# A DiT block with SSD and RG-LRU branches on one core: modulation one tile ahead, scans and Silus at other places

## The chip, the cores and the metric

One core of a Trainium2 chip. The metric is the device time of one execution in microseconds. TensorE (PE) multiplies matrices, VectorE (DVE) and ScalarE (ACT) work element by element, SyncE (SP) issues the loads, and 16 DMA engines carry them. Each engine executes its own instructions in the order in which they stand.

## The reference

One layer over 256 latent tokens with 256 context tokens, width 2048, fp32. Cut to what the change touches:

```python
mod = jax.nn.silu(c) @ w_ada + b_ada              # shift, scale and gate vectors
h = modulate(rmsnorm(x, norm_mix), sh_m, sc_m)    # h * (1 + scale) + shift
z, xs, bs, cs, dt_raw, xr, yr = split(h @ w_in)   # one input projection
# RG-LRU branch: r, i = sigmoid(gates(conv(xr))); a = exp(-8 * r * softplus(-lam))
#   u = sqrt(1 - a**2) * i * xr; bidirectional linear scan of (a, u)
# SSD branch: xs, bs, cs = silu(conv(...)); dt = softplus(dt_raw + bias)
#   y = chunked scan with exp(cumsum(dt * A)), 32 heads, 4 groups
out = (g_s * (ssd @ w_out_ssd) + g_r * (lru @ w_out_lru)) @ w_o
x = x + g_m * out; then modulate, SwiGLU FFN, gated residual, final rmsnorm
```

The context tokens use the same weights, and of them only the final states of the two scans are needed.

## The kernel before

Channels lie on the 128 partitions, so the width is 16 tiles (KT = 16); latent and context tokens stand side by side in 512 columns. Weights arrive in fp32 and are split on the chip: ScalarE casts a high part `wh` from `raw`, VectorE subtracts to a low part `wl`. A product is three matmuls: high by high, high by low, low by high. The activations have the same two parts, `T1` and `T2`.

**First stage (L324 to L413).** X is loaded and squared, and the sums of squares give `r1`, the reciprocal root mean square. Then for each tile k: `ada_sums(k)` multiplies the conditioning vectors by the modulation weights of the tile (four loads `wa` of 512 KB, 32 small matmuls, L344), `ada_turn(k)` copies the sums (`ra`) and transposes them, `modulated(k)` works out scale and shift, then `tt` (VectorE, L371), `T1` (ScalarE, L372) and `T2` (VectorE, L373). `slice_prep(k)` loads a weight slice `raw0` of 448 KB (seven column blocks, L381) and splits it into `wh0` and `wl0`. `main(k)` multiplies seven column blocks, three matmuls each (L391 to L393): a group below is such a block's three matmuls. The first stage's TensorE and SyncE orders are those of the program text; the orders of ScalarE and VectorE are chosen by the scheduler. `wa` has six buffers.

**Later stages.** `run` works through jobs (a weight block of 128 columns each). Behind every job's evacuation it runs one list of `turns` (`in_turn(n, f)` puts f n jobs ahead) and one step of the background list `bg`. In the LRU stage two tiles make a batch (`lru_batch`): `operands`, `gates` (matmuls `lg`, Sigmoids), `decays` (Exp and Tanh) and `scans` (Sqrt of `E`, then the scans). In the SSD stage six jobs (xs x4, B, C) make a group; behind the last one come the Silus of B, C and XS, the transposes (`pB`, `px`), the product `pC`, and four units. A unit fetches the cumulated decays (`AC`), builds `E` and `G` (L804, L813), takes two exponentials, multiplies (`operands`), and feeds 24 small matmuls `py` (`products`, L833).

ScalarE holds one set of function tables at a time, and changing the set is an instruction of its own (ACT_TABLE_LOAD, recorded at L107). `fn` (L105) chains all activations that need tables in the order of the program text.

Of the kernel before, what the change touches and what calls it, by code (L numbers as in the profile page):

```python
# [8 lines left out]
F32 = mybir.dt.float32  # L9
# [46 lines left out]
def hybrid_block(  # L56
# [62 lines left out]
    def lru_ps(name):  # L119
        return ps_tile("lru", name, 2)  # L120
# [206 lines left out]
    ssq = lru_ps("ssq")  # L327
    for k in range(0, KT, 2):
        sq = sp.tile([P, 2, 2 * T], F32, tag="sq2", name="sq", bufs=2)
        act.activation(sq, X[:, k:k + 2, :], AF.Square)  # L330
        dve.tensor_tensor(sq[:, 0], sq[:, 0], sq[:, 1], ALU.add)
        pe.matmul(ssq, ones, sq[:, 0], start=k == 0, stop=k == KT - 2)
    r1 = rstd_of(ssq, 2 * T, "r1", sp)
# [3 lines left out]
    def ada_sums(j):  # L337

        pa = ras[j] = lru_ps("pa")
        for q in range(4):  # L340
            w = sp.tile([P, 4, 2 * P], F32, tag="wa", name="wa", bufs=6)
            nc.sync.dma_start(w, w_ada_m[j, :, 4 * q:4 * q + 4, :])
            for g in range(4):
                pe.matmul(pa[32 * g:32 * g + 32, :2 * P], C[:, 4 * q + g, :], w[:, g, :],  # L344
                          start=q == 0, stop=q == 3, tile_position=(0, 32 * g))
# [10 lines left out]
    def modulated(j):  # L356
# [11 lines left out]
        for s in range(2):  # L368
# [4 lines left out]
            dve.scalar_tensor_tensor(T2[:, j, sl], tt[:, sl], sh, T1[:, j, sl].bitcast(F32),  # L373
                                     ALU.add, ALU.subtract)
# [20 lines left out]
    with tc.manual_schedule(engines={mybir.EngineType.PE, mybir.EngineType.SP}):  # L395
        ada_sums(0)
        ada_turn(0)
        hl = {0: slice_prep(0)}
        modulated(0)
        ada_sums(1)  # L400
        ada_turn(1)
        for k in range(KT):
            if k + 1 < KT:
                hl[k + 1] = slice_prep(k + 1)
                modulated(k + 1)
            main(k, range(5))
            if k + 2 < KT:
                ada_sums(k + 2)
            main(k, range(5, N0))
            if k + 2 < KT:  # L410
                ada_turn(k + 2)
            del hl[k]
# [3 lines left out]
    dve.tensor_scalar(lt[3], col("lam", 0, 32), -1.0, None, ALU.mult)  # L416
# [92 lines left out]
    def lru_batch(tiles):  # L509
# [42 lines left out]
        def scans():  # L552
# [4 lines left out]
            for t in tiles:  # L557
# [15 lines left out]
        todo = [(False, [lambda: operands(t0)]), (False, before[:]), (False, [lambda: gates(t0), lambda: operands(t1)]),  # L573
                (False, []), (True, [lambda: gates(t1), decays])]
# [23 lines left out]
    def dt_evac(ps):  # L598
# [13 lines left out]
        def steps(part):  # L612
# [11 lines left out]
            if part == 0:  # L624
# [9 lines left out]
                fn(ex[:, :P], ex[:, :P], AF.Exp)  # L634
                dve.tensor_tensor(ex[f, :P], ex[f, :P], dt[f, 0:P], ALU.mult)
                dve.tensor_tensor(ex[b, :P], ex[b, :P], dt[b, P:2 * P], ALU.mult)
                cols = (dt[:, :P], dt[:, P:], ac[:, :P], ac[:, P:], ex[:, :P])
            else:
                scan(ex[f, :T - 1][:, ::-1], da[f, 1:][:, ::-1], T - 1, f)
                scan(ex[b, 1:], da[b, :T - 1], T - 1, b)  # L640
                fn(ex, ex, AF.Exp)
                dve.tensor_tensor(ex, ex, dt, ALU.mult)
                cols = (ex[:, :P], ex[:, P:])

# [14 lines left out]
            return turn  # L659

        def first():
            turn0()
            in_turn(4, steps(1))

        turn0 = steps(0)
        in_turn(4, first)

# [24 lines left out]
    LONG = ((1, 2, 3), (4, 5, 6, 7), (2, 3, 4, 5), (3, 4, 5, 6))  # L692
    SHORT = ((2, 3, 5), (7, 9, 11, 13), (4, 6, 7, 9), (5, 7, 9, 11))

    def xs_evac(g, t):
        def f(ps):
# [6 lines left out]
            if t == 3:  # L703
                silus, *rest = ssd_group(g)
                silus()
                for ns, fs in zip(LONG if g < NG - 1 else SHORT, rest):
                    for n, part in zip(ns, fs):
                        in_turn(n, part)
        return f

    def ssd_group(g):
# [133 lines left out]
        return (silus, [context_tokens, context_states, carried_states], *zip(*units))  # L845
# [277 lines left out]
```

## Time and profile before

| | |
|---|---|
| time, median of 3 runs | 2028.81 us (2024.41 to 2029.35) |
| profiled execution | 2027.59 us, span 2025.8 us |
| mean granted clock of TensorE | 0.986 |
| busy: TensorE, VectorE, ScalarE | 97%, 71%, 54% of the span |
| DMA | 440.32 MB, mean 217 GB/s |
| table loads | 48 at L107, 1283 ns each |

The first stage ends about 139 us into the span, the LRU stage at some 520, the SSD groups at some 850; behind them come the remaining projections and the FFN. The span is that of the profiled execution; it is 1.8 us shorter than the execution's own time.

### The profile page before, as it was taken

How to read it: one execution, taken by the hardware profiler on the slowest of the kernel's cores; microseconds unless marked ns; L12 is line 12 of the kernel's file. 1: busy time of each engine (PE TensorE's matmuls, PEld its weight loads, DVE VectorE, ACT ScalarE, POOL GpSimd, SP SyncE). 2: the span in 40 equal slices, each digit the busy share in tenths (PEclk: the TensorE clock that was granted, in tenths of full speed). 3: DMA queues.
4: the chain of work that ended last, by engine and by line, in shares of the span. 5: the costliest groups of instructions: out<-in, count | busy, mean ns of one | idle time of the engine just before them, and what ended most of it. 6: DMA issues, size and time to landing. Idle time of an engine off the chain costs nothing.

```text
span 2025.8 us, 30510 instructions
## 1 busy us (share of the span) xinstructions
PE 1963.7 (97%) x11633; PEld 1691.9 (84%) x11633; DVE 1430.7 (71%) x2153; ACT 1088.2 (54%) x1652; POOL 0.2 (0%) x4
## 2 busy tenths in 40 slices
PE   7999899999999879999999999899999999999997
PEld 3778898898878769888888888788888888888887
DVE  5578989886776666888777878776666665545544
ACT  4245878684564454766655544554444444444442
POOL 0000000000000000000000000000000000000000
PEclk9999999999999989999999999999999999999999
DMA  9974354556454457899888877577777776666663
GB/s 371 358 271 144 122 160 132 170 170 199 140 160 143 138 164 228 264 315 360 290 274 274 271 249 254 175 249 232 231 241 237 230 230 189 184 188 186 185 193 122
DMA packets 143842, 440.32 MB, mean 217 GB/s; under 512 B 17488, under 2 KB 36176, under 8 KB 143568
## 3 DMA queue, kind: packets, MB, share of 16 engines
q1 hardware_dynamic: 143328, 437.91, 66.4%
q8 instruction: 91, 1.49, 0.3%
q10 hardware_dynamic: 368, 0.47, 0.1%
q14 instruction: 55, 0.45, 0.1%
HBM read 427.77 MB, written 10.55 MB: 216 GB/s over the span
## 4 chain that ended last, share of the span: by engine, by line
PE 92%; DMA 2%; DVE 2%; ACT 2%; issue 1%; SPq 0%; DVEq 0%; ACTq 0%
PE ps L206 36%; PE ps L209 19%; PE ps L188 5%; PE ps L189 5%; PE ps L190 5%; PE ps L192 3%; PE ps L193 3%; PE ps L194 3%; DMA AC<-acD 1%; PE ps L391 1%; PE pa L344 1%; PE ps L392 1%; PE py L833 1%; PE ps L393 1%; PE ps L228 1%; PE lg L535 1%
## 5 line engine op out<-in xcount | busy, mean ns | idle before, releaser
L174 DVE TENSOR_TENSOR wl<-raw,wh 128x1024 fp32r<-128x1024 f32 (+1 forms) x566 | 677.8, 1200 | 386.9 <-ACT wh L173 382.3
L173 ACT CAST wh<-raw 128x1024 fp32r<-128x1024 f32 (+1 forms) x566 | 581.0, 1030 | 646.8 <-issue 221.4
L206 PE MATMUL ps<-T,wh 128*128 128x512 f32 x3236 | 814.7, 393 | 0.0
L206 PEld LDWEIGHTS ps<-T,wh 128*128 128x128 f32 x3236 | 581.6, 189 | 105.2 <-issue 0.7
L209 PEld LDWEIGHTS ps<-T,wl 128*128 128x128 f32 x3236 | 442.7, 190 | 33.3
L209 PE MATMUL ps<-T,wl 128*128 128x256 f32 x3236 | 452.9, 282 | 0.0
L188 PE MATMUL ps<-T,wh 128*128 128x512 f32 x464 | 184.2, 397 | 0.0
L189 PE MATMUL ps<-T,wh 128*128 128x512 f32 x464 | 180.9, 390 | 0.0
L190 PE MATMUL ps<-T,wl 128*128 128x512 f32 x464 | 180.6, 389 | 0.0
L473 DVE SCALAR_TENSOR_TENSOR rawa<-rawa,sc 128x1024 f32<-128x1024 f32 x128 | 153.1, 1222 | 28.4 <-DMA rawa<-in_dram 28.1
L192 PE MATMUL ps<-T,wh 128*128 128x256 f32 x576 | 165.4, 287 | 0.0
L193 PE MATMUL ps<-T,wh 128*128 128x256 f32 x576 | 163.7, 284 | 0.0
L194 PE MATMUL ps<-T,wl 128*128 128x256 f32 x576 | 163.6, 284 | 0.0
L192 PEld LDWEIGHTS ps<-T,wh 128*128 128x128 f32 x576 | 111.3, 193 | 1.9 <-issue 0.7
L193 PEld LDWEIGHTS ps<-T,wh 128*128 128x128 f32 x576 | 111.4, 193 | 1.2 <-issue 0.5
L194 PEld LDWEIGHTS ps<-T,wl 128*128 128x128 f32 x576 | 111.2, 193 | 0.0
L188 PEld LDWEIGHTS ps<-T,wh 128*128 128x128 f32 x464 | 87.1, 188 | 20.5 <-issue 2.3
L189 PEld LDWEIGHTS ps<-T,wh 128*128 128x128 f32 x464 | 87.2, 188 | 18.9 <-issue 1.4
L190 PEld LDWEIGHTS ps<-T,wl 128*128 128x128 f32 x464 | 87.1, 188 | 18.5
L107 ACT ACT_TABLE_LOAD x48 | 61.6, 1283 | 0.8
L804 ACT ACTIVATE E<-AC,wt 128x128 f32<-128x128 f32 x64 | 20.6, 391 | 61.8 <-DMA AC<-acD 61.8
L385 DVE TENSOR_TENSOR wl<-raw,wh 128x896 fp32r<-128x896 f32 x16 | 17.5, 1092 | 45.1 <-ACT wh L384 45.1
(236 smaller groups left out, 1881.8 us busy)
## 6 DMA issues: line engine op xcount, KB each, us to landing
raw<-in_dram SPq DMA_DIRECT2D x534, 512.0 KB, 4.5
rawa<-in_dram SPq DMA_DIRECT2D x128, 512.0 KB, 5.9
wa<-in_dram SPq DMA_DIRECT2D x64, 512.0 KB, 7.2
AC<-acD SPq DMA_DIRECT2D x16, 512.0 KB, 6.6
raw<-in_dram SPq DMA_DIRECT2D x16, 448.0 KB, 7.1
raw<-in_dram SPq DMA_DIRECT2D x16, 384.0 KB, 3.3
raw<-in_dram SPq DMA_DIRECT2D x18, 256.0 KB, 2.7
X<-in_dram SPq DMA_DIRECT2D x8, 512.0 KB, 7.2
```

Of the source, the lines that this page charges most:

```text
L107: i = act.activation(dst, src, func, **kw).ins
L173: act.copy(h[:, :n], raw[:, :n])
L174: held["low"] = dve.tensor_sub(l[:, :n], raw[:, :n], h[:, :n].bitcast(F32)).ins
L188: pe.matmul(ps, wh, T1[:, k, :], start=s, stop=False)
L189: pe.matmul(ps, wh, T2[:, k, :], start=False, stop=False)
L190: pe.matmul(ps, wl, T1[:, k, :], start=False, stop=e)
L192: pe.matmul(ps[:, :T], wh, T1[:, k, :T], start=s, stop=False)
L193: pe.matmul(ps[:, :T], wh, T2[:, k, :T], start=False, stop=False)
L194: pe.matmul(ps[:, :T], wl, T1[:, k, :T], start=False, stop=e)
L206: pe.matmul(ps, wh, job.act(k), start=s, stop=False, skip_group_check=True)
L209: pe.matmul(ps[:, T:], l[:, i % KP, :], job.act(i)[:, :T], start=False, stop=i == last, skip_group_check=True)
L473: i = dve.scalar_tensor_tensor(raw, raw, 1.0, sc[:, h * 1024:h * 1024 + 1024], ALU.mult, ALU.mult, accum_out=MP[:, n, h:h + 1]).ins
```

## The change

Five pieces. (1) The squares go through the four `raw` buffers instead of two of their own, and stand ahead in the hand-written order; the Sqrt table is loaded early; the reciprocal is taken in two halves. (2) `wa` gets a seventh buffer, and sums, turn and modulation of a tile are done one tile ahead of its `main` instead of two; the groups of `main(k)` are spread around them. The softplus of `lam` waits for the modulation of tile 8. (3) In the LRU stage the `scans` of the batch before move from ahead of `gates(t0)` to behind it. (4) The softplus and scans of dt are spread over more turns. (5) The Silus of an SSD group go into the turn list behind the job, where the exponentials of the last unit of the group before stand already, instead of straight into the evacuation; and of the group before the last the last unit's products come one turn later.

```diff
@@ -324,13 +324,20 @@
     dve.memset(C, 0.0)
     fn(C[:, :, 0], col("c", 0, KT), AF.Silu)
     fn(C[:, :, 1], col("cc", 0, KT), AF.Silu)
-    ssq = lru_ps("ssq")
-    for k in range(0, KT, 2):
-        sq = sp.tile([P, 2, 2 * T], F32, tag="sq2", name="sq", bufs=2)
-        act.activation(sq, X[:, k:k + 2, :], AF.Square)
-        dve.tensor_tensor(sq[:, 0], sq[:, 0], sq[:, 1], ALU.add)
-        pe.matmul(ssq, ones, sq[:, 0], start=k == 0, stop=k == KT - 2)
-    r1 = rstd_of(ssq, 2 * T, "r1", sp)
+    fn(junk, epsb[:, 0:1], AF.Sqrt)
+    r1 = sp.tile([P, 2 * T], F32, name="r1")
+
+    def square_sums():
+
+        ssq = lru_ps("ssq")
+        for k in range(0, KT, 2):
+            sq = wp.tile([P, 2, 2 * T], F32, tag="raw", name="sq", bufs=RING)
+            act.activation(sq, X[:, k:k + 2, :], AF.Square)
+            dve.tensor_tensor(sq[:, 0], sq[:, 0], sq[:, 1], ALU.add)
+            pe.matmul(ssq, ones, sq[:, 0], start=k == 0, stop=k == KT - 2)
+        fn(r1, ssq, AF.Sqrt, bias=epsb[:, 0:1], scale=1.0 / D)
+        for s in range(2):
+            dve.reciprocal(r1[:, s * T:s * T + T], r1[:, s * T:s * T + T])
 
     ras = {}
 
@@ -338,7 +345,7 @@
 
         pa = ras[j] = lru_ps("pa")
         for q in range(4):
-            w = sp.tile([P, 4, 2 * P], F32, tag="wa", name="wa", bufs=6)
+            w = sp.tile([P, 4, 2 * P], F32, tag="wa", name="wa", bufs=7)
             nc.sync.dma_start(w, w_ada_m[j, :, 4 * q:4 * q + 4, :])
             for g in range(4):
                 pe.matmul(pa[32 * g:32 * g + 32, :2 * P], C[:, 4 * q + g, :], w[:, g, :],
@@ -370,8 +377,9 @@
             sc, sh = MA[:, s, j:j + 1], MA[:, 2 + s, j:j + 1]
             dve.scalar_tensor_tensor(tt[:, sl], X[:, j, sl], sc, r1[:, sl], ALU.mult, ALU.mult)
             act.activation(T1[:, j, sl], tt[:, sl], AF.Identity, bias=sh)
-            dve.scalar_tensor_tensor(T2[:, j, sl], tt[:, sl], sh, T1[:, j, sl].bitcast(F32),
-                                     ALU.add, ALU.subtract)
+            i = dve.scalar_tensor_tensor(T2[:, j, sl], tt[:, sl], sh, T1[:, j, sl].bitcast(F32),
+                                         ALU.add, ALU.subtract)
+        held["mod", j] = i.ins
 
 
     ps0 = [mm_ps("ps0") for _ in range(3)] + [lru_ps("ps0")] + [ssd_ps("ps0") for _ in range(3)]
@@ -393,27 +401,29 @@
             pe.matmul(ps0[n], l[:, n, :], T1[:, k, :], start=False, stop=k == KT - 1)
 
     with tc.manual_schedule(engines={mybir.EngineType.PE, mybir.EngineType.SP}):
+        square_sums()
         ada_sums(0)
         ada_turn(0)
         hl = {0: slice_prep(0)}
         modulated(0)
-        ada_sums(1)
-        ada_turn(1)
         for k in range(KT):
+
+            n = (N0, 4, 2)[k] if k < 3 else 1
+            main(k, range(n))
             if k + 1 < KT:
+                ada_sums(k + 1)
                 hl[k + 1] = slice_prep(k + 1)
+                main(k, range(n, min(n + 1, N0)))
+                ada_turn(k + 1)
                 modulated(k + 1)
-            main(k, range(5))
-            if k + 2 < KT:
-                ada_sums(k + 2)
-            main(k, range(5, N0))
-            if k + 2 < KT:
-                ada_turn(k + 2)
+            main(k, range(n + 1 if k + 1 < KT else n, N0))
             del hl[k]
 
 
     lt = [sp.tile([P, 32], F32, name=f"lt{i}") for i in range(4)]
-    dve.tensor_scalar(lt[3], col("lam", 0, 32), -1.0, None, ALU.mult)
+    i = dve.tensor_scalar(lt[3], col("lam", 0, 32), -1.0, None, ALU.mult).ins
+    tc.add_manual_dep(i, held["mod", 8].name, mybir.DependencyInfo(
+        mybir.DependencyClass.NoSync, mybir.DependencyReason.DATA), reason="first tiles first")
     log1p_exp(lt[3], lt[3], lt[:3])
     for i, m in enumerate((-LRU_C, LRU_C)):
         dve.tensor_scalar(SL[:, i, :], lt[3], m, None, ALU.mult)
@@ -570,8 +580,8 @@
 
 
         t0, t1 = tiles
-        todo = [(False, [lambda: operands(t0)]), (False, before[:]), (False, [lambda: gates(t0), lambda: operands(t1)]),
-                (False, []), (True, [lambda: gates(t1), decays])]
+        todo = [(False, [lambda: operands(t0)]), (False, []),
+                (False, [lambda: gates(t0), lambda: operands(t1)] + before), (False, []), (True, [lambda: gates(t1), decays])]
         before[:] = [scans]
         if tiles[1] == KT - 1:
             todo.append((False, [scans]))
@@ -631,16 +641,20 @@
                 for c in range(2):
                     for d, pr in enumerate((f, b)):
                         side.dma_start(acD[c, d], ac[pr, c * P:c * P + P])
-                fn(ex[:, :P], ex[:, :P], AF.Exp)
-                dve.tensor_tensor(ex[f, :P], ex[f, :P], dt[f, 0:P], ALU.mult)
-                dve.tensor_tensor(ex[b, :P], ex[b, :P], dt[b, P:2 * P], ALU.mult)
                 cols = (dt[:, :P], dt[:, P:], ac[:, :P], ac[:, P:], ex[:, :P])
             else:
                 scan(ex[f, :T - 1][:, ::-1], da[f, 1:][:, ::-1], T - 1, f)
                 scan(ex[b, 1:], da[b, :T - 1], T - 1, b)
-                fn(ex, ex, AF.Exp)
-                dve.tensor_tensor(ex, ex, dt, ALU.mult)
                 cols = (ex[:, :P], ex[:, P:])
+
+            def weights():
+                if part == 0:
+                    fn(ex[:, :P], ex[:, :P], AF.Exp)
+                    dve.tensor_tensor(ex[f, :P], ex[f, :P], dt[f, 0:P], ALU.mult)
+                    dve.tensor_tensor(ex[b, :P], ex[b, :P], dt[b, P:2 * P], ALU.mult)
+                else:
+                    fn(ex, ex, AF.Exp)
+                    dve.tensor_tensor(ex, ex, dt, ALU.mult)
 
             def turn():
                 pt = ssd_ps("pt")
@@ -656,14 +670,17 @@
                     pd = ssd_ps("pd")
                     pe.matmul(pd[:, :64], ones[:64], dg, start=True, stop=True)
                     fn(dec, pd[:, :64], AF.Exp)
-            return turn
-
-        def first():
-            turn0()
-            in_turn(4, steps(1))
-
-        turn0 = steps(0)
-        in_turn(4, first)
+                else:
+                    return
+                begin(1)
+
+            in_turn(1, weights)
+            in_turn(3, turn)
+
+        def begin(part):
+            in_turn(1, lambda: steps(part))
+
+        begin(0)
 
     def start_ssd():
         flush()
@@ -689,8 +706,9 @@
 
 
 
-    LONG = ((1, 2, 3), (4, 5, 6, 7), (2, 3, 4, 5), (3, 4, 5, 6))
-    SHORT = ((2, 3, 5), (7, 9, 11, 13), (4, 6, 7, 9), (5, 7, 9, 11))
+    LONG = ((0,), (1, 2, 3), (4, 5, 6, 7), (2, 3, 4, 5), (3, 4, 5, 6))
+    LAST_LONG = LONG[:2] + ((4, 5, 6, 8),) + LONG[3:]
+    SHORT = ((0,), (2, 3, 5), (7, 9, 11, 13), (4, 6, 7, 9), (5, 7, 9, 11))
 
     def xs_evac(g, t):
         def f(ps):
@@ -701,9 +719,8 @@
             i = 4 * g + t
             conv(ps, sd["XS"][:, t, :].rearrange("p (s t) -> p s t", s=2), col("cw", 4 * i, 4), col("cb", i), 2)
             if t == 3:
-                silus, *rest = ssd_group(g)
-                silus()
-                for ns, fs in zip(LONG if g < NG - 1 else SHORT, rest):
+                when = LONG if g < NG - 2 else LAST_LONG if g < NG - 1 else SHORT
+                for ns, fs in zip(when, ssd_group(g)):
                     for n, part in zip(ns, fs):
                         in_turn(n, part)
         return f
@@ -842,7 +859,7 @@
             return products, fetch, operands
 
         units = [unit(u, c) for u in range(2) for c in range(2)]
-        return (silus, [context_tokens, context_states, carried_states], *zip(*units))
+        return ([silus], [context_tokens, context_states, carried_states], *zip(*units))
 
     jobs = [Job(w_dt, KT, "narrow", None, dt_evac)]
     for t in range(N0, KT):
```

What it does to the orders, at three places. First, ScalarE in the first stage, before. `raw0_297`, `ra_293` and `tt_308` belong to tile 2, the next three numbers (`ra_361`, `raw0_365`, `tt_376`) to tile 3.

```order
L384 CAST wh0_299<-raw0_297 128x896
L351 COPY ra_293<-pa_262 128x256
L372 ACTIVATE T1_94<-tt_308,MA_102 128x256 x2
L351 COPY ra_361<-pa_330 128x256
L384 CAST wh0_367<-raw0_365 128x896
L372 ACTIVATE T1_94<-tt_376,MA_102 128x256 x2
```

The same place after; `raw0_307` is the slice of tile 2, `tt_263` belongs to tile 1, `raw0_369` is the slice of tile 3, `tt_325` belongs to tile 2.

```order
L392 CAST wh0_309<-raw0_307 128x896
L379 ACTIVATE T1_94<-tt_263,MA_102 128x256 x2
L358 COPY ra_316<-pa_282 128x256
L392 CAST wh0_371<-raw0_369 128x896
L379 ACTIVATE T1_94<-tt_325,MA_102 128x256 x2
L358 COPY ra_378<-pa_344 128x256
```

The cast of a slice stood beside the same tile's `T1`; it now stands ahead of the `T1` of the tile before. VectorE follows suit; before (`tt_376` is tile 3, `raw0_433` tile 4):

```order
L365 TENSOR_SCALAR m_371<-m_371,V_74 128x2
L366 TENSOR_SCALAR MA_102<-m_371,V_74 128x2
L371 SCALAR_TENSOR_TENSOR tt_376<-X_73,MA_102,r1_141 128x256 x2
L373 SCALAR_TENSOR_TENSOR T2_95<-tt_376,MA_102,T1_94 128x256 x2
L385 TENSOR_TENSOR wl0_436<-raw0_433,wh0_435 128x896
```

And after (`tt_452` is tile 4, `raw0_502` the slice of tile 5):

```order
L373 TENSOR_SCALAR MA_102<-m_447,V_74 128x2
L378 SCALAR_TENSOR_TENSOR tt_452<-X_73,MA_102,r1_109 128x256 x2
L393 TENSOR_TENSOR wl0_505<-raw0_502,wh0_504 128x896
L380 SCALAR_TENSOR_TENSOR T2_95<-tt_452,MA_102,T1_94 128x256 x2
L368 TENSOR_REDUCE m_515<-pa_477 128x4
```

The low part `wl0` of the next tile's slice has moved from behind `T2` to ahead of it. Second, ScalarE at the first SSD boundary, before. `AC_5368` and `E_5480` are the last unit of a group, `XS_4920` the next group's input, `E_5803` its first unit.

```order
L446 ACTIVATE XS_4920<-pad1_4503,V_74 128x512
L804 ACTIVATE E_5803<-AC_5719,wt_1277 128x128 x4
L173 CAST wh_5529<-raw_5455 128x1024
L107 ACTIVATE XS_4920<-XS_4920 128x2048
L107 ACT_TABLE_LOAD
L107 ACTIVATE AC_5368<-AC_5368 128x1024
L107 ACTIVATE E_5480<-E_5480 128x512
L107 ACTIVATE AC_5719<-AC_5719 128x1024
L107 ACTIVATE E_5803<-E_5803 128x512
```

After; `E_5479`, `G_5480` and `AC_5370` are the last unit of that group.

```order
L821 ACTIVATE E_5479<-AC_5370,wt_1279 128x128 x4
L830 ACTIVATE G_5480<-U_4958,wt_1279 128x128 x4
L107 ACTIVATE AC_5370<-AC_5370 128x1024
L107 ACTIVATE E_5479<-E_5479 128x512
L107 ACT_TABLE_LOAD
L107 ACTIVATE B_5228<-B_5228 128x512
L107 ACTIVATE Cm_5025<-Cm_5025 128x256
L173 CAST wh_5421<-raw_5343 128x1024
L173 CAST wh_5456<-raw_5419 128x1024
L452 COPY pad1_4505<-ps_5394 128x2x256
L456 ACTIVATE XS_4922<-pad1_4505,V_74 128x512
```

The exponentials of the last unit stood behind the Silu of XS and a table load; they now follow its own `E` and `G`, and the load and the Silus come behind them. Third, ScalarE in the LRU stage, before: `E_1826` and `E_1835` are a batch's two tiles, `R_2001` is the next batch's first gate.

```order
L107 ACT_TABLE_LOAD
L107 ACTIVATE E_1826<-E_1826,epsb_91 128x1024
L173 CAST wh_2124<-raw_2091 128x1024
L438 COPY pad2_1287<-ps_1933 128x4x64
L440 COPY pad2_1287<-ps_1933 128x256
L173 CAST wh_2157<-raw_2122 128x1024
L107 ACTIVATE E_1835<-E_1835,epsb_91 128x1024
L107 ACT_TABLE_LOAD
L107 ACTIVATE R_2001<-lg_2003,V_74 128x512
L107 ACTIVATE I_2002<-lg_2008,V_74 128x512
```

After; `E_1786` and `E_1795` are the batch, `R_1959` the next one's first gate.

```order
L107 ACT_TABLE_LOAD
L107 ACTIVATE R_1959<-lg_1961,V_74 128x512
L107 ACTIVATE I_1960<-lg_1966,V_74 128x512
L107 ACTIVATE R_1959<-lg_1971,V_74 128x512
L532 CAST lh_1983<-lw_1981 128x512
L107 ACTIVATE I_1960<-lg_1976,V_74 128x512
L534 CAST xh_1985<-xc_1314 128x512
L107 ACT_TABLE_LOAD
L107 ACTIVATE E_1786<-E_1786,epsb_91 128x1024
L107 ACTIVATE E_1795<-E_1795,epsb_91 128x1024
```

The Sqrt of the two tiles has moved behind the Sigmoids of the next batch's first tile, and one table load a batch is added; the run has eight more in all.

## Rows read from the trace of the kernel before

In a timeline the columns are start in us, duration in us, engine, line, operation, output and inputs, count, and in brackets the idle time before it with what ended it.

**Rows 1.** Page, part 4: shares of the chain by engine.

```profile
PE 92%; DMA 2%; DVE 2%; ACT 2%; issue 1%; SPq 0%; DVEq 0%; ACTq 0%
```

**Rows 2.** Waits of TensorE over the span: total, times, longest us.

```profile
PE py L833 <- DVE G L816: 24.9, 4, 11.6
...
PE lg L535 <- ACT R L107: 7.2, 2, 5.3
```

**Rows 3.** Windows view, first stage: span, PE, PEld, DVE, ACT, POOL, clock, DMA, GB/s.

```profile
60.00:80.00 20.00, 20.00 (x161) 13.82 (x160) 9.39 (x23) 6.43 (x12) 0.00 (x0) 1.00 0.98 360
```

**Rows 4.** Timeline, one tile of the first stage: start, us.

```profile
111.44 1.93 PE L344 MATMUL pa<-wa,C 128*32 128x256 f32 x32
112.14 0.80 SPq L342 DMA_DIRECT2D wa<-in_dram  x2
...
113.77 0.94 ACT L384 CAST wh<-raw 128x896 fp32r<-128x896 f32 x1
...
114.74 1.09 DVE L385 TENSOR_TENSOR wl<-raw,wh 128x896 fp32r<-128x896 f32 x1 [3.30 <-ACT wh L384]
...
117.68 0.88 DVE L373 SCALAR_TENSOR_TENSOR T<-tt,MA,T 128x256 fp32r<-128x256 f32 x2 [0.18 <-ACT T L372]
...
118.00 0.39 PE L392 MATMUL ps<-T,wh 128*128 128x512 f32 x1
...
118.54 1.93 PE L344 MATMUL pa<-wa,C 128*32 128x256 f32 x32
```

**Rows 5.** Landing of 512 KB loads issued by L157, from 200 to 300 us.

```profile
DMA to landing us min/median/max: 3.4/3.8/5.7
```

**Rows 6.** Landing of the first stage's slices, from 45 to 62 us.

```profile
DMA to landing us min/median/max: 6.2/6.6/7.0
```

**Rows 7.** Timeline: the first matmul of main(0).

```profile
28.52 0.48 PE L391 MATMUL ps<-T,wh 128*128 128x512 f32 x1
```

**Rows 8.** Timeline of ScalarE at the first SSD boundary.

```profile
578.79 1.28 ACT L804 ACTIVATE E<-AC,wt 128x128 f32<-128x128 f32 x4 [6.13 <-DMA AC<-acD]
...
581.94 1.92 ACT L107 ACTIVATE XS<-XS 128x2048 f32<-128x2048 f32 x1 [0.93 <-DVE XS L448]
583.86 1.28 ACT L107 ACT_TABLE_LOAD   x1
585.16 1.06 ACT L107 ACTIVATE AC<-AC 128x1024 f32<-128x1024 f32 x1
```

**Rows 9.** Timeline of TensorE: `py` at three boundaries, `px` at the first.

```profile
588.13 0.70 PE L833 MATMUL py<-G,xt 128*64 128x128 f32 x4 [5.05 <-DVE G L816]
...
592.65 1.09 PE L736 MATMUL px<-K,XS 128*128 128x128 f32 x6
...
671.77 0.69 PE L833 MATMUL py<-G,xt 128*64 128x128 f32 x4 [6.37 <-DVE G L816]
...
754.61 0.70 PE L833 MATMUL py<-G,xt 128*64 128x128 f32 x4 [11.62 <-DVE G L816]
```

**Rows 10.** Windows view behind five waits, columns as in Rows 3.

```profile
200.00:204.00 4.00, 4.00 (x13) 3.17 (x13) 1.82 (x3) 3.97 (x6) 0.00 (x0) 0.58 0.00 0
220.00:224.00 4.00, 3.31 (x8) 2.65 (x9) 4.00 (x6) 3.40 (x6) 0.00 (x0) 0.50 0.34 123
590.00:600.00 10.00, 10.00 (x79) 9.67 (x76) 8.10 (x20) 5.17 (x12) 0.00 (x0) 0.84 0.55 144
670.00:680.00 10.00, 8.23 (x69) 7.90 (x70) 8.71 (x15) 5.73 (x11) 0.00 (x0) 0.74 0.37 78
755.00:765.00 10.00, 10.00 (x76) 9.67 (x73) 2.52 (x4) 1.39 (x2) 0.00 (x0) 0.73 0.26 81
```

**Rows 11.** Timeline of ScalarE in the LRU stage.

```profile
217.49 1.15 ACT L107 ACTIVATE E<-E,epsb 128x1024 f32<-128x1024 f32 x1 [1.15 <-DVE E L549]
218.65 1.28 ACT L107 ACT_TABLE_LOAD   x1
```

## The prediction

> **What bounds the kernel now.** I read the page's chain first: TensorE carries 92% of it [rows 1], so only what TensorE waits for, or does at a lower clock, can be won or lost. The waits of TensorE come next [rows 2]: of the large ones, the SSD products `py` wait 24.9 us in four places for VectorE's `G`, and the gate products `lg` 7.2 us in two places for ScalarE. Then the stretches. In the first stage TensorE is busy 20.00 us of 20 while the DMA engines are busy 0.98 of the time at 360 GB/s [rows 3]: two limits lie side by side there. One tile of that stage runs from one start of the modulation's sums to the next, 111.44 to 118.54, 7.10 us, and TensorE fills it [rows 4].
>
> **The first stage.** The part to follow is where the next weight slice stands. In the order shown above, ScalarE casts the raw slice of tile k+1 before it writes T1 of tile k, and VectorE makes `wl` of k+1 before T2 of tile k. With seven `wa` buffers the fourth `wa` of tile k+1 takes the buffer that the first quarter of sums(k) frees, and the slice `raw0` of k+1 is issued right behind it on SyncE. So, with S the start of sums(k), everything hangs on one line:
> - S+0.70: the `wa` is issued (before: sums 111.44, issue 112.14 [rows 4]).
> - It lands after some 3.6 us; the lower and middle landings of a 512 KB load in a stretch with room are 3.4 and 3.8 [rows 5]. The 448 KB behind it take 459/360 = 1.27 us at the rate of [rows 3], some of it overlapped, so 1.2. The slice is there at S+5.5.
> - From the cast to `wl` 0.97 (113.77 to 114.74), `wl` 1.09, of which 1.05 until the next instruction, T2 0.88; then L392 and L393 of the one group that stands ahead of the next sums, which start 0.54 behind L392 (118.00 to 118.54) [rows 4], 0.6 with the semaphore. Together 3.5. The next sums start at S+9.0.
>
> TensorE has 7.10 us of work in a period, so 1.9 us are lost; nothing would be lost if the slice landed by S+3.6, which even the shortest landing of [rows 5] forbids. There are 14 periods. In the first, tile 0 leaves no group to do and four groups of tile 1 stand ahead of the sums: 5.0 us of work in 9.0+2.1, 6.0 lost. In the second, five groups: 5.7 in 9.0+0.7, 4.0 lost. Twelve more lose 1.9 each, 22.8. In all 32.8. Against it: main(0) starts earlier than its 28.52 [rows 7]. With squares in four buffers, the Sqrt table loaded ahead, and the softplus out of the way I put it at 25.7, 2.8 earlier, but sums(1), 2.2 us with their switch, lay ahead of it before and lie behind it now: -0.6. **Stage: +32.** Bounds: the slice lands with the `wa`, 3.4 after its own issue 0.42 later: S+4.5, period 8.0, 12 x 0.9 + 5 + 3 - 0.6 = +18. Or the landing is 0.7 longer: +32 + 14 x 0.7 = +42. The queue should be nearly empty at S+0.7, since the 7.1 us of transfers of a period, issued together behind S+0.7, end before S+9.7; that is why I don't take the 6.2 to 7.0 that `raw0` took in the full queue [rows 6].
>
> A page's price for the same landing: the Trainium skill, "DMA: Bandwidth & Descriptors", section on the anatomy of one DMA, gives a fixed 2.0 us plus bytes/436 GB/s, so by estimate 4.25 us for the two loads together, the slice at S+4.95, and the sum 8 us lower. The rows here run above that price: 3.4 to 3.8 where it gives 3.2.
>
> The clock: after a stall of 1.9 us the granted clock was 0.58 for four us [rows 10]. Four us at 0.58 are 1.7 us of work, and the period has 1.9 us in reserve, so most of it is hidden: +2 (0 to 10, the far end if the low clock lasts the whole period in a third of the tiles). The held softplus of lambda costs one more table load in a ScalarE that idles there: nothing.
>
> **The SSD boundaries.** Three times the last unit of a group is late: `py` started at 588.13 after 5.05 us, 671.77 after 6.37, 754.61 after 11.62 [rows 9], 23.0 together. At the first, ScalarE had made `E` at 578.79 but then waited for the convolution, ran the long Silu of `XS` (1.92) and a table load (1.28), and only then, at 585.16, the exponentials [rows 8]. Now the exponentials stand right behind `E` and `G`: E's four instructions take 1.28 [rows 8], G's as much by estimate, so the first exponential starts near 581.3; from there to `py` it took 2.97 (585.16 to 588.13), so `py` can start at 584.3, and TensorE comes at 583.1. So 1.2 stays of 5.05, and I keep 0.5 at the other two together (at the third, one more gate product now stands ahead of `py`): -21.3. The waits also cost clock: 0.84, 0.74 and 0.73 in the ten us behind them, with 10.0, 8.2 and 10.0 us busy [rows 10]: 1.6 + 2.1 + 2.7 = 6.4. **Sum: -28.** The Silus come later. `px`, which needs the one of `XS`, started 4.5 us behind `py` at the low clock [rows 9], so some 2.3 at the full one: near 586.6. Exponentials until about 583, load and Silu 3.2: `XS` is there at 586.2, just in time. Bounds: -30 all gone, -20 if `XS` is some 2.5 us late at each.
>
> **The LRU stage.** `Sqrt` of the batch before stood at 217.49 ahead of the next Sigmoids and waited for VectorE; then came a table load, and the gates waited 5.3 us behind them [rows 2, 11]; the other 1.9 was behind the softplus of dt on VectorE, now split over turns. The clock afterwards was 0.58 over 4.0 us and 0.50 over 3.3 [rows 10]: 1.7 + 1.7. All of it would be 10.6; I take **-9**, since the dt pieces now switch tables between gates and one may be late. Bounds -3 (only the clock's share) to -11. Eight more table loads a run cost 8 x 1.28 = 10.3 us of ScalarE (load 583.86, next instruction 585.16 [rows 8]), hidden where it has room: it is busy 54% of the span, though 3.97 and 3.40 of 4 us in the two stretches above [rows 10]; without that cover the whole 10.3 would come back.
>
> The Trainium skill speaks against this part: "ScalarE: Activation LUTs", section on what a table load costs, adds a drain of 1.38 us to each load, so by estimate 21 us of ScalarE for the eight, and its section on table sets asks for batching by set. The row shows the next instruction 0.02 us behind the load, so the trace has no such drain.
>
> **Sum.** Profiled execution 2027.59 (1.2 below the median of the runs): 2027.6 + 32 + 2 - 28 - 9 = 2024.6; I say 2024. That lies within 0.3% (6.1 us) of the median 2028.8, about the least that a measurement of this kernel tells from no change.
>
> **The rivals.**
> - *Slice in time, faster.* The raw slice isn't queued behind the `wa` but lands with it. For it: sixteen engines share both transfers. Against: 7.1 us of transfers a tile at 360 GB/s leave little free. Stage +18 or less: 2010. Beside it: the Trainium skill ("DMA: Bandwidth & Descriptors", section on queues, rings and completion order) says that completion isn't first in, first out on one issuing engine. No row here shows two loads overtaking.
> - *Slice late, slower.* It takes 6.6 us from its own issue as in the full queue [rows 6]: S+7.7, period 11.2, 2.2 more than forecast, +31: 2055. It decides (slower than 2034.9) from 0.8 us a tile, a slice later than S+6.3.
> - *The waits only move.* At the boundaries `px` waits for `XS` instead and the clock falls all the same: half the gain, 2038.
> - *The reorder does nothing in the LRU.* The extra table loads put the gates as late as the Sqrt did: 2033.
>
> **Chances.** Forecast 0.58 (own range 2014 to 2034), slice in time 0.12, slice late 0.15, waits move 0.10, no LRU gain 0.05. Faster by over 0.3% (below 2022.7): 0.22 of the forecast's and the 0.12, 0.34. Within: 0.32 of the forecast's, 0.04 each of the last two, 0.40. Slower: 0.04, 0.15, 0.06 and 0.01, 0.26. Adding the far ends of the terms, 18 - 30 - 11 and 42 + 7 - 20 - 3, gives 2005 to 2054; I leave a little of both tails out: 2004 to 2047.
>
> **What would show it.** In the first stage: sums of neighbouring tiles 9.0 us apart and not 7.1, TensorE waiting some 1.9 us in each for T2, ScalarE waiting for `raw0` at each cast, DMA share near 0.8; the LRU stage begins near 170. At the boundaries `py` waits under 1.5 us and no Silu stands between `E` and its exponentials; `lg` no longer waits 5.3. The prediction is wrong if the sums stay 7.1 apart, if a boundary shows `px` waiting for `XS`, or if the granted clock of the first stage falls over whole tiles.

## The result, and the profile after

The changed kernel takes 2061.28 us in the median, the kernel before 2029.08 on the same chip: a ratio of 1.0162, 95% interval 1.0142 to 1.0182. It is slower by 1.6%, and the time lies above the range that was given. One of the four executions fell into a slower state (2199.52 us); the median is of all four, the ratio of the other three. The profiled execution took 2062.07 us, its span is 2060.3. Where the time went, by the start of a stage's first and last instructions in the two traces:

| stage, from and to | before | after | difference |
|---|---|---|---|
| first stage, to the first matmul behind it | 0 to 138.8 | 0 to 198.8 | +60.1 |
| LRU stage, to the first `pB` | to 509.7 (370.9) | to 568.2 (369.4) | -1.6 |
| SSD stage, first `pB` to last `py` | to 843.7 (334.0) | to 878.7 (310.5) | -23.5 |
| the rest, to the end of the span | to 2025.8 (1182.1) | to 2060.3 (1181.6) | -0.5 |

Waits of TensorE after, which answer to [rows 2] (us in total, times, longest). Line numbers are those of the changed kernel: L399 to L401 are the groups of `main`, L379 is T1, L380 T2, L662 the dt transposes, L753 `px`, L850 `py`.

```profile
PE ps L399 <- ACT T L379: 33.8, 12, 6.9
...
PE pt L662 <- DVE dt L657: 8.0, 1, 8.0
PE ps L400 <- DVE T L380: 7.6, 14, 0.6
...
PE px L753 <- ACT XS L107: 4.1, 2, 2.5
...
PE py L850 <- DVE G L833: 0.9, 1, 0.9
```

The `lg` wait of 7.2 us is gone and `py` has 0.9 of its 24.9; in their place stand 41.4 us behind T1 and T2 in the first stage and one new wait of 8.0 in the LRU stage. The 33.8 fell on T1, where the forecast had put the waits on T2: both stand behind the late slice, T1 behind its cast on ScalarE, T2 behind its low part on VectorE. The chain through one period of the first stage, and the start of the next (start, us, what), to be read beside [rows 4]:

```profile
59.87 1.06 PE pa L351 x8
...
60.94 0.33 SPq L349
...
61.36 4.94 DMA raw<-in_dram
...
66.32 0.95 ACT wh L392
...
67.29 1.09 DVE wl L393
68.39 0.80 DVE T L380 x2
...
69.97 0.61 PE pa L351 x8
...
70.60 0.33 SPq L349
...
71.02 6.44 DMA raw<-in_dram
...
77.48 0.95 ACT wh L392
...
78.45 1.09 DVE wl L393
79.54 0.81 DVE T L380 x2
...
81.61 0.57 PE pa L351
```

The links are those of the forecast, one by one: a quarter of the sums, the `wa` issue, the slice `raw0`, its cast, `wl` of the next tile, T2, the next sums. Only the landing is longer: 4.94 and 6.44 us from the slice's issue, where 4.4 had been put. ScalarE's waits over the stage, and the landing of its slices (L389) from 45 to 190 us, answer to [rows 5, 6]:

```profile
ACT wh L392 <- DMA raw<-in_dram: 49.4, 13, 5.3
```

```profile
DMA to landing us min/median/max: 4.5/5.3/6.6
```

The windows view of the stage, with columns as in [rows 3]: 20 us of it, and the two stretches from the issue of the first `wa` or of the slice to the slice's landing.

```profile
60.00:80.00 20.00, 14.83 (x105) 9.10 (x97) 6.72 (x18) 4.24 (x8) 0.00 (x0) 0.93 0.75 255
```

```profile
60.94:66.30 5.36, 5.36 (x41) 3.53 (x33) 1.64 (x6) 0.37 (x1) 0.00 (x0) 0.94 0.83 261
71.02:77.46 6.44, 5.36 (x36) 3.72 (x28) 1.64 (x6) 0.37 (x1) 0.00 (x0) 1.00 0.87 274
```

TensorE is busy 14.83 us of 20 at a mean clock of 0.93. In the second fence, 5.36 us at 261 GB/s are 1.40 MB, but the `wa` and the slice are 0.98 MB; in the next line 6.44 us at 274 GB/s are 1.76 MB. So 0.4 to 0.8 MB of the three loads issued behind the slice had been carried before it landed, 1.2 to 2.2 us at 360 GB/s.

The two slices differ in one thing more, the time that SyncE's issue of the slice took (start, us):

```profile
61.36 0.38 SPq L389 DMA_DIRECT2D raw<-in_dram  x1
...
71.02 0.88 SPq L389 DMA_DIRECT2D raw<-in_dram  x1
```

Of the 13 slices, eight were issued in 0.38 us and landed after 4.5 to 5.6 us; five took 0.82 to 1.82 us to issue and landed after 6.2 to 6.6. What held those issues no run shows.

### The profile page after: what moved, and what is told of

It is laid out like the page before. It is cut to its first block, busy times and chain, and to the rows that moved or that the text cites. A ratio compares the mean times of both kernels' runs of the same rounds, so it can differ in the third digit from the quotient of the medians.

```text
span 2060.3 us, 30564 instructions
## 1 busy us (share of the span) xinstructions
PE 1977.5 (96%) x11633; PEld 1691.5 (82%) x11633; DVE 1428.3 (69%) x2154; ACT 1096.2 (53%) x1661; POOL 0.2 (0%) x4
## 3 DMA queue, kind: packets, MB, share of 16 engines
q8 instruction: 91, 1.49, 0.3%
## 4 chain that ended last, share of the span: by engine, by line
PE 84%; DMA 6%; DVE 5%; ACT 3%; issue 1%; SPq 0%; DVEq 0%; ACTq 0%
PE ps L206 35%; PE ps L209 18%; PE ps L188 4%; PE ps L189 4%; PE ps L190 4%; DMA raw<-in_dram 4%; PE ps L192 3%; PE ps L193 3%; PE ps L194 3%; DMA AC<-acD 2%; PE ps L228 1%; DVE wl L174 1%; DVE wl L393 1%; PE ps L400 1%; ACT wh L392 1%
## 5 line engine op out<-in xcount | busy, mean ns | idle before, releaser
L206 PE MATMUL ps<-T,wh 128*128 128x512 f32 x3236 | 813.9, 393 | 0.0
L206 PEld LDWEIGHTS ps<-T,wh 128*128 128x128 f32 x3236 | 581.0, 189 | 104.9 <-issue 0.3
L188 PE MATMUL ps<-T,wh 128*128 128x512 f32 x464 | 184.9, 399 | 0.0
L189 PE MATMUL ps<-T,wh 128*128 128x512 f32 x464 | 181.3, 391 | 0.0
L192 PEld LDWEIGHTS ps<-T,wh 128*128 128x128 f32 x576 | 111.1, 193 | 1.5 <-issue 0.4
L193 PEld LDWEIGHTS ps<-T,wh 128*128 128x128 f32 x576 | 111.2, 193 | 1.2 <-issue 0.5
L188 PEld LDWEIGHTS ps<-T,wh 128*128 128x128 f32 x464 | 87.5, 189 | 20.9 <-issue 2.1
L189 PEld LDWEIGHTS ps<-T,wh 128*128 128x128 f32 x464 | 87.5, 189 | 19.1 <-issue 1.4
L399 PE MATMUL ps<-T,wh 128*128 128x512 f32 x112 | 51.0, 455 | 33.9 <-ACT T L379 33.8
L399 PEld LDWEIGHTS ps<-T,wh 128*128 128x128 f32 x112 | 22.3, 199 | 49.9 <-ACT T L379 39.6
```

Source lines behind the costliest of these rows:

```text
L188: pe.matmul(ps, wh, T1[:, k, :], start=s, stop=False)
L189: pe.matmul(ps, wh, T2[:, k, :], start=False, stop=False)
L192: pe.matmul(ps[:, :T], wh, T1[:, k, :T], start=s, stop=False)
L193: pe.matmul(ps[:, :T], wh, T2[:, k, :T], start=False, stop=False)
L206: pe.matmul(ps, wh, job.act(k), start=s, stop=False, skip_group_check=True)
L399: pe.matmul(ps0[n], h[:, n, :], T1[:, k, :], start=k == 0, stop=False)
```

## The experiments

Each run's ratio is to the kernel before on the same chip. "Stage end" is the first matmul behind the first stage.

**The slice issued earlier.** One line is moved, and two dependencies keep ScalarE's and VectorE's orders as they were in the changed kernel.

```diff
-                ada_sums(k + 1)
                 hl[k + 1] = slice_prep(k + 1)
+                ada_sums(k + 1)
```

> The changed kernel with raw0 of tile k+1 issued ahead of its four wa instead of behind them; the orders of ScalarE and VectorE are those of the changed kernel (the cast still stands ahead of T1 of the tile before). Theory A, the late slice behind the wa that waits for the sums holds ScalarE: the sums come 7.1 to 7.9 us apart again, TensorE's first matmul behind the first stage comes at 146 to 158 instead of 198.8, time 2010 to 2022. Rival B, the modulation one tile ahead is itself too long a chain (sums, turn, tt, T1, T2 in one period): the sums stay over 9.5 apart, time over 2042. Rival C, the low clock of the stage makes half of the loss: some 30 us come back, time near 2030.

2023.18 us, ratio 0.9979 (0.9970 to 0.9988); stage end 159.8. A piece of the chain of this run:

```profile
82.69 0.19 DVE m L368
...
83.96 0.48 DVE tt L378
84.44 1.00 DVE wl L393
85.44 0.80 DVE T L380 x2
...
86.28 0.50 PE ps L404
...
87.02 0.99 PE pa L351 x14
```

The slice is in no link any more: its lateness was the cause, and 39 us of the stage come back. The sums are 7.42 apart (79.60 to 87.02 in the same chain) and not 7.10, since `wl` of the next tile, 1.00, still stands between `tt` and T2. The time misses the expected 2022 by 1 us and the stage end 158 by 2. From the sums of tile 1 on the first three periods are long (11.6, 9.1 and 8.0 us), and so is the last (9.7); the start is taken up below, the last period stays open.

**The cast behind T1.** The slice stays late; the cast of tile k+1 on ScalarE waits for T1 of tile k, and its low part on VectorE for T2.

```diff
+        if k > 1:
+            for i, o in ((c, held["t1", k - 1]), (d, held["mod", k - 1])):
+                tc.add_manual_dep(i, o.name, ...)
```

> The changed kernel with the cast of the next slice held behind T1 of the tile before, and its low part behind T2; the slice is still issued behind the wa. Theory A (head of the line): as late as the slice is, it holds nothing that is due, sums 7.1 to 7.6 apart, first matmul behind the stage at 144 to 152, time 2006 to 2016. Rival B (the chain of the modulation is too long): over 9.5 apart, time over 2042. Rival C (clock): near 2030.

2012.74 us, ratio 0.9929 (0.9913 to 0.9946); stage end 149.0. The sums in its chain, and the slices' landing (L389, from 45 to 190 us):

```profile
65.34 1.86 PE pa L351 x32
...
72.43 1.86 PE pa L351 x32
...
79.52 1.86 PE pa L351 x32
...
86.61 1.86 PE pa L351 x32
```

```profile
DMA to landing us min/median/max: 5.0/5.9/7.6
```

The period is 7.09 with slices that land later (median 5.9) than in the changed kernel (5.3). A late slice costs nothing where nothing due stands behind its cast: theory A holds, B and C fall.

**Eight `wa` buffers.**

```diff
-            w = sp.tile([P, 4, 2 * P], F32, tag="wa", name="wa", bufs=7)
+            w = sp.tile([P, 4, 2 * P], F32, tag="wa", name="wa", bufs=8)
```

> The changed kernel with eight buffers of wa instead of seven, so that the last wa of tile k+1, and the slice behind it, waits for the sums of tile k-1 and no longer for those of tile k. Theory A (the seventh buffer's gate makes the slice late): sums 7.1 to 7.5 apart, time 2010 to 2024, much as with the slice issued earlier. Rival: the slice is late because the queue is full whatever the gate; sums stay over 9 apart, time over 2040.

2031.36 us, ratio 1.0021 (1.0009 to 1.0033); stage end 171.7. Neither expectation was met. Waits of TensorE:

```profile
PE pa L360 <- ACT ra L358: 14.9, 11, 4.2
```

With the buffer the scheduler put the cast one place further ahead, in front of `ra` of the tile before, and the slice (7.6 us to landing in the median) now holds the copy that the transposes wait for. The late slice still stands ahead of something due: the wait has moved from T1 to this copy.

**The loads behind the slice held back.** A small copy on ScalarE behind the cast writes the first `wa` of the next tile, so that SyncE issues it late.

```diff
+            if q == 0 and j > 1:
+                act.copy(w[:, 0, :1], hl[j - 1][0][:, 0, :1].bitcast(F32))
             nc.sync.dma_start(w, w_ada_m[j, :, 4 * q:4 * q + 4, :])
```

> The changed kernel, in which the first wa of the next tile is written by one small copy on ScalarE behind the cast of the slice, so that SyncE issues the loads behind the slice only when the slice has landed. Read from tile 8 on, where ScalarE's order is that of the changed kernel with the small copy added. Theory D (the loads behind the slice share the engines with it, and that is what the prediction's landing lacked): the slice lands 4.4 to 4.9 us after its issue and not 5.6 in the median, the sums are 9.2 to 10.2 apart and not 11.0. Rival E (the landing has another reason, as the latency of the load ahead): it stays at 5.4 or more, and the period at 10.8 or more.

2054.13 us, ratio 1.0127 (1.0107 to 1.0148). From tile 8 on the sums were 10.4 apart in the mean, but from 115 us on the slice took 7.2 us in the median. The held loads now lie ahead of the next slice, all five issued within 2 us, so from tile 8 on the run tells neither theory's case.

One earlier tile does. The slice of tile 2 has one `wa` ahead of it, issued 0.42 us before, and in this run nothing behind it until it has landed:

```profile
L391 SPq DMA_DIRECT2D raw<-in_dram x1: 1551/1551/1551, 35.6 to 35.6; - x1
...
DMA to landing us min/median/max: 5.6/5.6/5.6
```

The same slice in the changed kernel, with the three loads behind it:

```profile
L389 SPq DMA_DIRECT2D raw<-in_dram x1: 1487/1487/1487, 35.3 to 35.3; - x1
...
DMA to landing us min/median/max: 6.8/6.8/6.8
```

The issues took about as long (1.55 and 1.49 us), and the slice landed 1.3 us sooner without the followers (5.56 and 6.84). In two other runs with the followers it took 6.6 us (the cast behind T1) and 7.5 (dt one turn later). So theory D holds for this tile, 1.0 to 1.9 us by one slice without followers against three with them. For the other tiles it is argued from the bytes alone.

**The old first stage** under everything else of the change: squares, buffers, loop and softplus as before.

```diff
-        for k in range(KT):
-
-            n = (N0, 4, 2)[k] if k < 3 else 1
-            main(k, range(n))
...
+            main(k, range(5))
+            if k + 2 < KT:
+                ada_sums(k + 2)
+            main(k, range(5, N0))
+            if k + 2 < KT:
+                ada_turn(k + 2)
```

> The changed kernel with the whole first stage of the kernel before (squares in two buffers, six wa, modulation two tiles ahead, softplus early). If the parts add up, the first stage gives back its 60 us and the rest keeps its gain of some 26: time 2000 to 2005, first matmul behind the stage at 138.8. If the later gain hung on the first stage (its slices, its clock), the time is above 2010.

2002.61 us, ratio 0.9878 (0.9862 to 0.9894); stage end 137.6, LRU stage 370.5, SSD stage 309.5. The parts add up. It is the base of four runs below.

**The new squares with the old loop** (on the base of the best mix, below): four buffers, the Sqrt table early, the reciprocal in halves, the softplus held, six `wa`.

```diff
     with tc.manual_schedule(engines={mybir.EngineType.PE, mybir.EngineType.SP}):
+        square_sums()
         ada_sums(0)
```

> The best mix with the new squares (four buffers, ahead in the hand-written order, Sqrt table early, reciprocal in halves, softplus held), but the old loop two tiles ahead with six wa. Theory: the first tile's start hangs on the loads of wa and X, which run at 0.96 to 1.0 of the DMA engines until 40 us, so the squares' part is worth little: first matmul behind the stage at 136 to 140.5, time 1990 to 1996. Rival: with the sums of tiles 0 and 1 behind the squares in TensorE's order, the start comes later: 143 or more, time over 1997.

1994.74 us, ratio 0.9840 (0.9824 to 0.9857); stage end 140.0. Its like with the old squares had 140.6: this part is worth nothing that shows.

**The Silus first again** on the old first stage.

```diff
-                for ns, fs in zip(when, ssd_group(g)):
+                (silus,), *rest = ssd_group(g)
+                silus()
+                for ns, fs in zip(when[1:], rest):
```

> The changed kernel with the old first stage, and the Silus of an SSD group back in the evacuation, ahead of the exponentials of the unit before; all else as with the old first stage (2002.6). Theory: the Silus' place alone makes the gain at the boundaries; py waits some 5, 6 and 6 to 12 us again, the SSD stage (first pB to last py) grows from 309.5 to 328 to 334, time 2020 to 2027. Rival: the later product of the last unit makes much of it, then the stage stays under 325 and the time under 2017.

2020.78 us, ratio 0.9965 (0.9954 to 0.9977); SSD stage 328.4.

```profile
PE py L842 <- DVE G L825: 19.8, 4, 7.0
```

The place of the Silus is worth 18.2 us of time, 18.8 of the stage, and `py` has 19.8 us of its waits back.

**The last unit not later**, on the old first stage.

```diff
-    LAST_LONG = LONG[:2] + ((4, 5, 6, 8),) + LONG[3:]
+    LAST_LONG = LONG
```

> The changed kernel with the old first stage, and the last unit's products of the group before the last in the old turn; all else as with the old first stage (2002.6). Theory: with the Silus behind, the exponentials of that unit come right behind its E, but the AC load lands when TensorE has already come, so py waits some 5 us there with the clock low behind it: time 2008 to 2012. Rival: the Silus' place alone suffices, time within 3 us of 2002.6.

2001.25 us, ratio 0.9868 (0.9854 to 0.9883), SSD stage 307.5, as the rival said. With the Silus behind, the later turn is worth nothing.

**The scans at their old place**, on the old first stage.

```diff
-        todo = [..., (False, []), (False, [lambda: gates(t0), lambda: operands(t1)] + before), ...
+        todo = [..., (False, before[:]), (False, [lambda: gates(t0), lambda: operands(t1)]), ...
```

> The changed kernel with the old first stage, and the scans of the LRU batch ahead of the gates again; all else as with the old first stage (2002.6). Theory: Sqrt ahead of the Sigmoids waits for VectorE again in the first batches, lg waits some 5 us with the clock low behind it, against eight table loads less that nobody waited for: time 2007 to 2011. Rival: with dt split the Sqrt is no longer late, so the move is worth nothing: within 3 us of 2002.6; or the table loads cost TensorE something, then it is faster.

1991.65 us, ratio 0.9823 (0.9808 to 0.9838): 11 us faster where the theory wanted 5 to 8 slower. LRU stage 360.8. The wait of 8.0 has shrunk, and no `lg` wait came back. Waits of TensorE, and the second half's dt exponential on ScalarE:

```profile
PE px L743 <- ACT XS L107: 3.5, 2, 3.0
...
PE pt L652 <- DVE dt L647: 0.9, 1, 0.9
```

```profile
238.79 0.42 ACT L107 ACTIVATE dt<-dt 64x256 f32<-64x256 f32 x1 [1.18 <-DVE dt L614]
```

**dt two turns later**, on the old first stage, and **one turn later** in the changed kernel (2 and 4 in place of 3 and 5).

```diff
-            in_turn(1, weights)
-            in_turn(3, turn)
+            in_turn(3, weights)
+            in_turn(5, turn)
```

> The changed kernel with the old first stage, the dt weights and their transposes two turns later each. Theory: the 8.0 us wait of TensorE behind the dt exponential goes entirely (one turn later left 3.3 of it), with the clock behind it: LRU stage (first matmul behind the first stage to first pB) 360 to 363 instead of 370.5, time 1993 to 1997. Rival: the wait moves to the next Sigmoids or to the boundary with SSD: time within 4 us of 2002.6.

1992.77 us, ratio 0.9826 (0.9810 to 0.9843), LRU stage 359.8; the 8.0 us wait is gone. This run keeps the added table loads, 54 in place of 50 with the scans at their old place, so they are not what made that run faster.

> The changed kernel with the exponential of the dt weights and their transposes one turn later each. Theory: in the changed kernel the second half's exponential waits for VectorE's scans on ScalarE, the Sigmoids stand behind it, and TensorE waits 8.0 us once with the clock low behind it; with a turn more that wait goes, and the time falls by 8 to 11 us to 2050 to 2054. Rival: the wait only moves to another turn's matmuls, time within 3 us of the changed kernel's 2061.

2054.34 us, ratio 1.0127 (1.0105 to 1.0150); LRU stage 364.6. Of the 8.0 us wait 3.3 are left:

```profile
PE pt L662 <- DVE dt L657: 3.3, 1, 3.3
```

The time fell by 7 us and not by 8 to 11, and the LRU stage gave only 4.7 of it. In this profile the first stage, whose code is that of the changed kernel, ended at 195.0 and not at 198.8, with one slow issue of a slice in place of five and a median landing of 4.9.

**The split of dt alone**, and **the move of the scans alone**, each in the kernel before: the diff's parts on `steps` and on `todo`, one without the other.

> The kernel before with the split of the dt steps alone. Theory from the last runs: the LRU stage's whole gain is the split's (with the scans at their old place the stage took 360.8 and lg waited nowhere): LRU stage near 361 instead of 370.9, time 2016 to 2020. Rival: the split pays only with the other changes; lg still waits 5 us for the Sqrt, time above 2022.

2016.71 us, ratio 0.9946 (0.9932 to 0.9961); LRU stage 360.8, no `lg` wait. The split alone makes the LRU gain.

> The kernel before with the move of the scans behind the gates alone (dt in its old form). The prediction's reading: the 5.3 us wait of lg behind the Sqrt goes with its clock, time 2020 to 2024. Rival: the softplus of dt keeps VectorE late, so the wait only moves to another instruction of the same stretch: within 4 us of the kernel before, 2024 to 2032.

2025.22 us, ratio 0.9986 (0.9977 to 0.9995); LRU stage 369.8. Waits of TensorE:

```profile
PE ps L192 <- ACT gt L487: 3.4, 1, 3.4
...
PE ps L188 <- ACT pad L440: 2.5, 1, 2.5
PE lg L535 <- ACT R L107: 1.9, 1, 1.9
```

The rival holds: the 5.3 us wait only moved, to 3.4 and 2.5 us behind ScalarE's copies `gt` and `pad`.

**The best mix**: the old first stage, the scans at their old place, and dt one turn later.

```diff
+            in_turn(2, weights)
+            in_turn(4, turn)
```

> Old first stage, scans at their old place, dt split with weights and transposes one turn later, Silus behind the exponentials. Theory: the 0.9 us wait left behind dt goes, everything else as with the scans at their old place (1991.7): time 1989 to 1993. Rival: moving the dt turns makes another wait in the LRU stage, time above 1995.

1995.18 us, ratio 0.9836 (0.9822 to 0.9850), slower than expected by 2 us and at the edge of the rival's 1995; its interval overlaps that of the run with the scans at their old place. The rival is not borne out: the LRU stage took 360.8 in both profiles, and the 1.8 us lie in the first stage (140.6 and 138.8), which is the same code. The version that beats both kernels is: old first stage, old place of the scans, dt split, Silus behind the exponentials, 1991.65 us, 1.8% below the kernel before; dt two turns later with the scans moved (1992.77) is not told apart from it.

## Why the prediction was wrong

**The first stage: the mechanism right, the size wrong.** The forecast was +32 and +2 for the clock; it cost +60, 26 more. The LRU stage brought 7 less than was forecast and the boundaries 4.5 less: together some 37 us, those between 2024 and 2061. The terms that failed in the first stage:
- The landing. "It lands after some 3.6 us ... The slice is there at S+5.5" took the middle of [rows 5] and 1.2 behind it, 4.4 us from the slice's own issue. It measured 5.3 in the median, and 5.6 in the mean of the twelve slices that the sum prices alike: 1.2 us a tile, 15 us in all. The text asked what lay ahead of the slice in the queue; what lay behind it was left out. At tile 2 the loads behind cost 1.0 to 1.9 us, by one slice without them. How much of the 1.2 is theirs elsewhere is open: the slices with a short issue exceed 4.4 by 0.6 in the mean, the five with a long one by 2.1, and nearly all had three loads behind. The price that the prediction quotes beside its own from the Trainium skill ("DMA: Bandwidth & Descriptors", section on the anatomy of one DMA) is a fit to loads issued from GpSimd, while SyncE issues these. Its 4.25 us for both loads compares with a shortest of 4.96 here (4.54 behind the 0.42 between the two issues).
- The clock. "Most of it is hidden" overlooked that two links of the chain itself are TensorE's: the first quarter of the sums (1.06 us where it ran at the low clock, 0.61 else) and the last two matmuls of the group (1.2 us from T2's end at 80.35 to the sums at about 81.5, against 0.7). By estimate from these that is some 0.5 us in every period that held a low stretch. In 60:80 the clock was 0.93.
- The start. main(0) came at 27.64 and not at 25.7, and ran at the low clock behind a wait of 4.4 us for T1, which the sums of tile 1 had filled before. The sums of tile 1 began at 34.20 where the sum had 25.7 and seven groups of 0.69, 30.5: +3.7. The late start, with the first two periods short of groups, stays in both mended versions, whose stages end 11 and 22 us behind the old one's 137.6.

```profile
27.64 0.79 PE L399 MATMUL ps<-T,wh 128*128 128x512 f32 x1 [4.40 <-ACT T L379]
...
34.20 1.93 PE L351 MATMUL pa<-wa,C 128*32 128x256 f32 x32
...
187.76 1.93 PE L351 MATMUL pa<-wa,C 128*32 128x256 f32 x32
```

Periods: 153.6 us from the sums of tile 1 to those of tile 15 (34.20 to 187.76), forecast 128.8, +24.8, of which 4.8 in the first two and 20 in the other twelve (10.7 each and not 9.0). With the +3.7 that is the 28 by which 60 exceeds 32. The rival "slice late" had the right case and the wrong reason (a full queue); that its 2055 comes near is partly luck, since its period of 11.2 was too long and it kept the -28 and -9. The range's upper end added 7 us for the clock where the text gives the term up to 10; with 10 it would be 2057 before the tails, still too low.

**The LRU stage: wrong.** "I take -9" gave the `lg` wait of 5.3 to the move of the scans and 1.9 to dt. The runs turn this round: the move alone saves 1.1 us of the stage, the split alone 10. Both together save 1.6. With both, VectorE runs the batch's scans among the first steps of the second half's softplus of dt: those steps (up to the first product behind the reciprocal) took 12.3 us with the old first stage, and 5.2 with the scans at their old place. So the scans of dt end later, the dt exponential on ScalarE waits for them, and the Sigmoids stand behind it. This is read from the two traces; no run changes VectorE's order alone. ScalarE in the changed kernel:

```profile
306.69 0.42 ACT L107 ACTIVATE dt<-dt 64x256 f32<-64x256 f32 x1 [6.14 <-DVE dt L624]
307.12 1.28 ACT L107 ACT_TABLE_LOAD   x1
308.42 0.69 ACT L107 ACTIVATE R<-lg,V 128x512 f32<-128x512 f32 x1
```

The 6.14 us idle behind the dt scans, 1.18 with the scans at their old place, is what became TensorE's 8.0. The forecast had said "one may be late", as a share of 1.6 us. The added table loads were not seen to cost TensorE time: the stage took 359.8 in a run with 54 loads (dt two turns later) and 360.8 in one with 50 (scans at their old place).

**The SSD boundaries: right, the size near.** -28 was forecast, -23.5 measured. `py` no longer waits there, as said. The 4.5 us missing are about the size of the waits of `px` for `XS` (4.1 in two places), a small form of the rival "the waits only move", which the text had called "just in time". The later turn of the last unit, counted as help at the third boundary, is worth nothing that shows.

## What to carry to other kernels

On an engine that takes its instructions in order, look at what stands directly ahead of each link of a loop: a cast whose load is still on the way there turned a 7.1 us period into one of 11, and putting it behind T1, and the low part behind T2, gave the period back with the load as late as ever. Price a load's landing with the loads behind it too, and ask a trace for its spread. And when two changes touch the order of the same engine, price them together: of two that each looked like a gain in the LRU stage, one was worth 10 us, the other 1, and the pair 2.

## What was not expected of the hardware

A 448 KB load with one 512 KB load ahead landed 4.5 to 6.6 us after its issue, median 5.3, while 0.4 to 0.8 MB of later loads were carried first (in the two places counted). The landings fell into two groups with the length of SyncE's own issue, 4.5 to 5.6 us behind 0.38 and 6.2 to 6.6 behind 0.82 to 1.82. In the one place where such a load had nothing behind it, it still took 5.6 us, and 6.6 to 7.5 with three behind. And the mean granted clock from 45 to 190 us was 0.90:

```profile
45.00:190.00 145.00, 115.02 (x751) 70.19 (x752) 50.03 (x139) 30.41 (x57) 0.00 (x0) 0.90 0.69 231
```

TensorE stalled 1.7 and 2.9 us for T1 in the two periods of the chain above, and the same 32 matmuls of the sums took 1.93 us in some periods and 2.80 to 3.64 in others.
